# A weight column turned before the first block of x, and the mixer's first casts moved one unit later

## The chip, the cores and the metric

The kernel runs on one core of one Trainium2 chip. The metric is the device time of one execution in microseconds (us), as a median of runs. Every time in this document comes from such runs or from the profile of one execution.

Five engines work at the same time, each through its own list of instructions in order: PE (TensorE: matrix products and transposes), DVE (VectorE), ACT (ScalarE), POOL (GpSimd) and SP (SyncE, which only issues loads here). In the rows of the profile PEld is the loading of a stationary operand of PE, and SPq, ACTq and POOLq are DMA issues.

## The reference, cut to what matters

One layer of a residual block over 512 rows of 1024 features, all in float32:

```python
h = h + 0.5 * swiglu(rmsnorm(h, ffn1_norm), ffn1_w_in, ffn1_w_out)     # first layer, d_ff = 2816
z = rmsnorm(h, mix_norm) @ w_in                                        # the mixer's projection
h = h + concat([conv_module(z...), gated_linear_attention(z...)]) @ w_out
h = h + 0.5 * swiglu(rmsnorm(h, ffn2_norm), ffn2_w_in, ffn2_w_out)
h = h + sigmoid(rmsnorm(h, ple_norm) @ w_g) * (p @ w_p)
out = rmsnorm(h, final_norm)
```

The change touches the first rows (the norm's weight `ffn1_norm`) and the passage from the first layer to the mixer's projection.

## The kernel before, in words

Activations are kept transposed: eight tiles `hT` of 128 features by 512 rows. Each product is made of three: both operands are split into a high part in a rounded format (`wh`, `hg` high, `wa` high) and the rest (`wl`, `hg` low), and high by high, high by low and low by high are summed in PSUM. So each block of weights costs a cast on ACT (the high part) and a subtraction on DVE (the low part). For some blocks the low part is made in another way, by the helper `added`: ACT writes the negated high part, and a DMA issued by POOL adds the raw weights to it in place ("the add" below, `wa<-wr` with POOLq in the rows). That takes work from DVE and gives it to POOL and the DMA engines.

**The opening.** `warm_up` (line 196) gives PE idle products, then `turn_x(0, turn_vec)` transposes the first block of x in four pieces, with the norm's weight row turned into a column (`turn`, line 183) between the second piece and the third. `split_x` then scales block 0 by that column into `hg` (ACT high, DVE low), and `take` begins the products with the first weights.

**The first layer.** `ffn` lists units of PE work, two accumulator halves at a time. For the last pair of columns (number 10) the units m5, m4 and m3 finish its accumulators. After m3, ACT copies half of the last accumulator out (`g<-pd`), DVE adds and scales it, ACT applies the silu (`s<-g`), DVE multiplies (`m<-u,s`), and ACT and DVE split it (`act`). The pieces of the second matrix follow: four column pairs n = 0, 2, 4, 6, each in two groups of rows. The second group of n = 0 is the first that needs the `act` of pair 10. After each column pair is done, DVE adds it to `hT`, ACT and DVE make the mixer's `hg` of these two blocks, and ACT squares them.

**What sets the order.** PE, DVE and ACT keep the order in which the code emits them (class `Ordered`, line 36); `drive` (line 667 on) emits each unit's casts some units ahead of its products. `hooks` (line 1033 on) hang extra work on units: `ahead` (line 271) loads two blocks of mixer weights, casts them (`high4`, line 276) and starts their adds. It hangs on m4 of pair 10 (two blocks, called W0 and W1 here) and on the piece called ("last", 4) (two more, W2 and W3). Behind the layer `in_order(True)` (line 1053) starts a new chain, and the casts of four more mixer blocks, B0, B1 (`raw_b`) and A0, A1 (`raw_a`, from line 1105 on), are scheduled among the layer's last instructions by a scheduler of the framework; they may come before an earlier written instruction on ACT.

**Slots.** All raw weights share six slots `wr`. SP issues the loads in written order, and each waits until the last reader of a freed slot is done. For a block with `added` the last reader is the add itself; for others it is DVE's subtraction.

Of the kernel before, what the change touches and what calls it, by code (L numbers as in the profile page):

```python
# [15 lines left out]
P = 128  # L16
SEQ = 512
D = 1024
DC = D // P
DFF = 2816  # L20
D_CONV = 512
# [41 lines left out]
def block_kernel(ctx: ExitStack, tc: tile.TileContext, a: dict, out: bass.AP):  # L63
    nc = tc.nc
# [25 lines left out]
    def bt2(dt=F32R, s="a"):  # L90
        t = big.tile([P, 2, SEQ], dt, tag="A", bufs=NA, name=nm(s))
        hi, lo = t[:, 0], t[:, 1]
        whole_of[id(hi)] = hi, t
        return hi, lo
# [32 lines left out]
    def bank():  # L127
        if mode[0] == 0:
            turn_no[0] += 1
            at = turn_no[0] % 7  # L130
            if at in (3, 4):
                return fixed()
            if at in (5, 6):
                return spare()
        return psum(singles(), 3, [P, SEQ])
# [16 lines left out]
    def aux():  # L152
        if mode[0] == 2:
            return fixed()
        return psum(singles(), 1, [P, SEQ], "aux")
# [11 lines left out]
    vecs = [("ffn1_norm", 8), ("mix_norm", 8), ("ffn2_norm", 8), ("ple_norm", 8),  # L167
            ("conv_b", 4), ("conv_ln_g", 4), ("conv_ln_b", 4), ("gate_b", 2), ("gla_norm", 4)]
# [3 lines left out]
    def columns(names, n, tile_name, queue):  # L172

        row = cp.tile([n, P], F32, name=tile_name + "r")
        col = cp.tile([P, n], F32, name=tile_name)
        r0 = 0
        for name, m in names:
            queue.dma_start(out=row[r0:r0 + m, :], in_=a[name][0].rearrange("(r p) -> r p", p=P))
            for c in range(m):
                vcols[name, c] = col[:, r0 + c:r0 + c + 1]  # L180
            r0 += m

        def turn():
            ps = aux()
            pe.transpose(ps[:, 0:n], row, ident[:n, :n])
            dve.tensor_copy(col, ps[:, 0:n])

        return turn
# [7 lines left out]
    def warm_up(n, zeroed=0):  # L196
        idle = bank()
        for _ in range(zeroed):
            pe.matmul(idle[:, 0:P], zeros, zeros, start=True, stop=True)
        for _ in range(n):  # L200
            pe.transpose(idle[:, 0:P], ident, ident)

    warm_up(7, 2)
    turn_vec = columns(vecs[:1], 8, "vcol1", nc.scalar)

    def split(src, s, alloc=bt):
        hi, lo = bt2(s=s) if alloc is bt else (alloc(F32R, s + "H"), alloc(F32R, s + "L"))
# [20 lines left out]
    def raw(nk, ncol):  # L228
        return wp.tile([P, 1024], F32, tag="raw", bufs=6, name=nm("wr"))[:, :nk * ncol].rearrange(
            "p (k c) -> p k c", k=nk)  # L230

    def fetch(r3, src, k0, nk, c0, ncol):
        nc.sync.dma_start(out=r3, in_=src[k0 * P:(k0 + nk) * P, c0:c0 + ncol].rearrange("(k p) c -> p k c", p=P))

    def load(src, k0, nk, c0, ncol):
        r3 = raw(nk, ncol)
        fetch(r3, src, k0, nk, c0, ncol)
        return r3
# [16 lines left out]
    def added(w):  # L255

        h3, l3, r3 = w
        act.mul(l3, r3, -1.0)
        pool.dma_start(out=l3.bitcast(F32), in_=r3, accum_op=ALU.add)
        return w  # L260
# [10 lines left out]
    def ahead(src, c0, ncol):  # L271


        return [[added(w) for w in high4(load(src, 0, DC, c, P))] for c in range(c0, c0 + ncol, P)]

    def high4(r3):

        w = []
        for k in range(0, DC, 4):
            hi, lo = (t.rearrange("p (k c) -> p k c", k=4) for t in bt2(s="wa"))  # L280
            act.copy(hi, r3[:, k:k + 4])
            w.append((hi, lo, r3[:, k:k + 4]))
        return w
# [247 lines left out]
    def turn_x(c, between=None):  # L531
        ps = bank()
        for t in range(TB):
            if between and t == 2:
                between()
            pe.transpose(ps[:, t * P:(t + 1) * P], xt[c][t], ident)
        xps.append(ps)
# [64 lines left out]
    nc.sync.dma_start(out=made[1], in_=a["conv_w"][0])  # L602
    for i in range(P // RANK):
        nc.sync.dma_start(out=made[2][i * RANK:(i + 1) * RANK, :], in_=a["gate_w_up"][0])
    turn_x(0, turn_vec)
    warm_up(4)
    ps0 = [fixed(), fixed()] + parted(double())
    split_w(0, 1, dve.tensor_copy, 2)
# [30 lines left out]
    def constants():  # L639
        _, cwrow, gwurow = made  # L640
        gwu = cp.tile([P, 2 * P], F32, name="gwu")
        act.copy(gwu, gwurow)
        cw = cp.tile([P, 4 * WIDTH], F32, name="cw")
        ps = aux()
        for c in range(4):
            pe.transpose(ps[:, c * WIDTH:(c + 1) * WIDTH], cwrow[:, c * P:(c + 1) * P], ident[:WIDTH, :WIDTH])
        dve.tensor_copy(cw, ps[:, 0:4 * WIDTH])
        mean = cp.tile([P, P], F32, name="mean")
        pool.memset(mean, 1.0 / D_CONV)
        m1, m2 = (bt(s="m1")[:, 0:4 * CH].rearrange("p (c t) -> p c t", t=CH) for _ in range(2))  # L650
        mask = cp.tile([P, 4, CH], I32, name="mask")
        pool.memset(m1, 1.0)
        pool.memset(m2, 1.0)
        pool.affine_select(out=m1, in_=m1, compare_op=ALU.is_gt, fill=0.0, base=0,
                           pattern=[[0, 4], [-1, CH]], channel_multiplier=1)
        pool.affine_select(out=m2, in_=m2, compare_op=ALU.is_gt, fill=0.0, base=-CH,
                           pattern=[[0, 4], [-1, CH]], channel_multiplier=1)
        pool.tensor_copy(mask[0:CH], m1[0:CH])
        pool.tensor_copy(mask[CH:P], m2[CH:P])
        nbias = cp.tile([P, 2], F32, name="nbias")  # L660
        for j in range(2):
            dve.tensor_scalar(nbias[:, j:j + 1], vec("gate_b", j), -1.0, None, ALU.mult)
        made[:] = cw, gwu, mean, mask, nbias
# [359 lines left out]
    w_in = a["w_in"][0]  # L1023
    w_ahead = []

    def sums_hooks(x, names, at):

        h = {}
        for name, key in zip(names, at):
# [6 lines left out]
                  ("h4", 1): lambda *_: [steps[4](), xb.split("t2")],  # L1036
                  ("h5", 1): lambda *_: [xb.split("t3"), w2.s12()]})
    hooks.update({("m5", 3): lambda *_: made[0](), ("m3", 3): lambda *_: constants(),
                  ("m4", 10): lambda *_: w_ahead.append(ahead(w_in, D_CONV, 2 * P)),
                  ("last", 4): lambda *_: w_ahead.append(ahead(w_in, 0, 2 * P))})  # L1040
    FAR = {("h5", 1): 3, ("m1", 2): 3}
    CASTS = {("h5", 1): 4, ("m1", 2): 4}
# [78 lines left out]
    rs, rsb = mid  # L1121
# [427 lines left out]
    for k in range(4):  # L1549
        for n in range(3):  # L1550
            w, ps = half[n]
# [329 lines left out]
    rs = norm.rows()  # L1881
# [98 lines left out]
```

## Time and profile before

| what | value |
|---|---|
| median of 3 runs | 934.87 us (934.66 to 935.77) |
| the profiled execution's own time | 934.95 us |
| its span in the profile | 933.1 us |
| granted clock of PE | 0.997 |
| DMA queues | q1: loads issued by SP; q0: DMAs issued by POOL |

A row of the timeline has the start in us, the time from the start of the first to the end of the last of the instructions merged in it, the engine, the line, the operation, `out<-in` by the program's names, the shape, the count, and in brackets the idle time of the engine before it with what ended it. Nearly all compute rows have line 46, since the class `Ordered` records them; the tile names tell them apart. A row of DMA issues has the time that the issuing engine took, not the transfer.

### The profile page before, as it was taken

What the parts mean: (1) busy time and instruction counts of PE and PEld (TensorE: products, weight loads), DVE (VectorE), ACT (ScalarE), POOL (GpSimd) and SP (SyncE); (2) the same over time, 40 slices, a digit from 0 to 9 for tenths busy, and PEclk for the clock granted to TensorE, in tenths of its full rate; (3) what the DMA queues carried; (4) which work ended last, traced back from release to release, by engine and by line L of the source; (5) the groups of instructions that cost most, each with busy time, mean ns of one, the idle gap of its engine ahead of it and who ended that gap; (6) DMA issues with size and microseconds to landing.
All of it is one profiled execution on the core that took longest, in us unless ns stands there. A gap on an engine that the chain in (4) does not pass through costs nothing.

```text
span 933.1 us, 12990 instructions
## 1 busy us (share of the span) xinstructions
PE 923.0 (99%) x5011; PEld 785.3 (84%) x5011; DVE 826.6 (89%) x1107; ACT 509.7 (55%) x745; POOL 56.9 (6%) x74
## 2 busy tenths in 40 slices
PE   9999999999999999999999999999999999999996
PEld 7898888888888878788877889888888888888885
DVE  6799989999999776999987789999999999997896
ACT  5874445445544574463564875355445444456883
POOL 0100100000000021001030020000000000000131
PEclk9999999999999999999999999999999999999998
DMA  7643333233432594346552654333223422348463
GB/s 231 186 112 113 116 113 113 74 108 113 124 87 66 153 237 116 77 111 161 137 124 79 158 115 134 113 113 116 89 90 122 126 89 79 110 132 245 92 111 115
DMA packets 108129, 114.37 MB, mean 123 GB/s; under 512 B 5203, under 2 KB 96517, under 8 KB 108068
## 3 DMA queue, kind: packets, MB, share of 16 engines
q1 hardware_dynamic: 101748, 94.67, 33.0%
q0 software_dynamic: 6304, 18.88, 11.2%
q8 instruction: 39, 0.64, 0.3%
q14 instruction: 22, 0.18, 0.1%
q10 hardware_dynamic: 16, 0.00, 0.0%
HBM read 93.61 MB, written 2.10 MB: 103 GB/s over the span
## 4 chain that ended last, share of the span: by engine, by line
PE 96%; DVE 2%; ACT 1%; DMA 1%; issue 0%; POOLq 0%; DVEq 0%; ACTq 0%
PE ps L46 58%; PE pd L46 38%; DMA wr<-in_w_in 1%; DVE wl L46 1%; DVE sq L46 0%; DVE g L46 0%; ACT act L46 0%; ACT wa L46 0%; ACT wh L46 0%; DVE u L46 0%; DVE rs L46 0%; ACT yc L46 0%; DVE y L46 0%; DVE s L46 0%; DVE act L46 0%
## 5 line engine op out<-in xcount | busy, mean ns | idle before, releaser
L46 DVE TENSOR_TENSOR wl<-wr,wh 128x1024 fp32r<-128x1024 f32 (+2 forms) x161 | 188.6, 1182 | 18.6 <-ACT wh L46 18.5
L46 ACT CAST wh<-wr 128x1024 fp32r<-128x1024 f32 (+2 forms) x178 | 176.4, 1022 | 21.6 <-PE ps L46 6.4
L46 PE MATMUL pd<-hg,wh 128*128 128x512 f32 x576 | 150.0, 391 | 0.0
L46 PE MATMUL ps<-act,wh 128*128 128x512 f32 x448 | 138.8, 391 | 0.5 <-ACT act L46 0.3
L46 PEld LDWEIGHTS pd<-hg,wh 128*128 128x128 f32 x576 | 106.1, 188 | 20.7 <-DVE u L46 0.3
L46 PE MATMUL ps<-hg,wh 128*128 128x512 f32 (+1 forms) x448 | 117.7, 347 | 0.1
L46 PE MATMUL pd<-t,wh 128*128 128x512 f32 x392 | 98.3, 393 | 0.0
L46 PEld LDWEIGHTS ps<-act,wh 128*128 128x128 f32 x448 | 83.1, 188 | 17.7 <-ACT act L46 0.7
L46 ACT ACTIVATE s<-g 128x512 f32<-128x512 f32 x48 | 30.3, 632 | 117.7 <-DVE g L46 117.7
L46 ACT COPY sq<-pd 128x1024 f32<-128x1024 f32 x45 | 45.8, 1017 | 86.7 <-PE pd L46 52.4
L46 PEld LDWEIGHTS ps<-hg,wh 128*128 128x128 f32 x448 | 78.0, 190 | 11.7 <-issue 1.3
L46 PE MATMUL ps<-act,wl 128*128 128x512 f32 x224 | 87.2, 389 | 0.0
L46 PE MATMUL pd<-hg,wl 128*128 128x256 f32 (+1 forms) x544 | 83.9, 289 | 0.0
L46 PEld LDWEIGHTS pd<-hg,wl 128*128 128x128 f32 x544 | 75.9, 190 | 6.3
L46 PEld LDWEIGHTS pd<-t,wh 128*128 128x128 f32 x392 | 70.6, 189 | 12.5
L46 PE MATMUL ps<-hg,wl 128*128 128x512 f32 (+1 forms) x224 | 77.1, 344 | 0.0
L46 ACT CAST wh<-sm 128x1024 fp32r<-128x1024 f32 x42 | 44.1, 1051 | 57.1 <-DVE sm L46 50.9
L46 DVE SCALAR_TENSOR_TENSOR cv<-glu,cw,cv 128x502 f32<-128x502 f32 (+24 forms) x90 | 61.9, 734 | 0.3
L46 PEld LDWEIGHTS pd<-t,wl 128*128 128x128 f32 x392 | 53.5, 191 | 3.8
L46 DVE TENSOR_TENSOR sq<-pd,sq 128x1024 f32<-128x1024 f32 x45 | 54.8, 1219 | 0.8 <-PE pd L46 0.8
L46 DVE TENSOR_TENSOR wl<-sm,wh 128x1024 fp32r<-128x1024 f32 x42 | 51.1, 1220 | 5.0 <-ACT wh L46 5.0
L46 PE MATMUL ps<-wh,hg 128*128 128x512 f32 x176 | 54.8, 393 | 0.0
(322 smaller groups left out, 1638.5 us busy)
## 6 DMA issues: line engine op xcount, KB each, us to landing
wr<-in_ffn_w_in SPq DMA_DIRECT2D x84, 512.0 KB
wr<-in_ffn_w_out SPq DMA_DIRECT2D x32, 512.0 KB
wr<-in_w_in SPq DMA_DIRECT2D x20, 512.0 KB
wl<-wr POOLq DMA_DIRECT2D x18, 512.0 KB, 5.2
wr<-in_ffn_w_out SPq DMA_DIRECT2D x16, 384.0 KB
wr<-in_w_out SPq DMA_DIRECT2D x8, 512.0 KB
wq<-in_ple_w_gate SPq DMA_DIRECT2D x8, 512.0 KB
wl<-wq POOLq DMA_DIRECT2D x8, 512.0 KB, 4.6
```

Source lines behind the costliest of these rows:

```text
L46: inst = call(*args, **kwargs)
```

## The change

Three edits:

1. The column of the first norm's weight is turned right after the idle products, ahead of all four pieces of x, and the identity turns of `warm_up` ahead of it go from seven to five.
2. The hook on m4 of pair 10 now only loads W0 and W1. Casting them and starting their adds is moved to the hook on m3 of pair 10, one unit later.
3. `ahead` is cut into loading and `prepared`, which casts; for W2 and W3 it does the same work as before.

```diff
-    warm_up(7, 2)
-    turn_vec = columns(vecs[:1], 8, "vcol1", nc.scalar)
+    warm_up(5, 2)
+    columns(vecs[:1], 8, "vcol1", nc.scalar)()
...
-        return [[added(w) for w in high4(load(src, 0, DC, c, P))] for c in range(c0, c0 + ncol, P)]
+        return prepared([load(src, 0, DC, c, P) for c in range(c0, c0 + ncol, P)])
+
+    def prepared(rs):
+
+        return [[added(w) for w in high4(r3)] for r3 in rs]
...
-    turn_x(0, turn_vec)
+    turn_x(0)
...
-                  ("m4", 10): lambda *_: w_ahead.append(ahead(w_in, D_CONV, 2 * P)),
+                  ("m4", 10): lambda *_: w_ahead.append([load(w_in, 0, DC, D_CONV + i * P, P) for i in range(2)]),
+                  ("m3", 10): lambda *_: w_ahead.append(prepared(w_ahead.pop())),
```

The order of PE differs only in the opening, and those of DVE and POOL do not differ. ACT differs in two places. The first is the end of the first layer. Of the names, `wa_3028` and `wa_3030` belong to W0 and `wa_3038` and `wa_3040` to W1, `g_537` is the copy out of the last accumulator, and the `wh` of 768 are blocks of the second matrix. ACT before:

```order
L46 CAST wa_3028<-wr_3026 128x512
L46 CAST wa_3030<-wr_3026 128x512
L46 ACTIVATE wa_3028<-wr_3026 128x512
L46 ACTIVATE wa_3030<-wr_3026 128x512
L46 CAST wa_3038<-wr_3036 128x512
L46 CAST wa_3040<-wr_3036 128x512
L46 ACTIVATE wa_3038<-wr_3036 128x512
L46 ACTIVATE wa_3040<-wr_3036 128x512
L46 CAST wh_3048<-wr_2942 128x768
L46 COPY g_537_3068<-pd_2842 128x512
```

ACT at the same place after the change:

```order
L46 CAST wh_3030<-wr_2940 128x768
L46 COPY g_533_3050<-pd_2840 128x512
L46 CAST wa_3054<-wr_3024 128x512
L46 CAST wa_3056<-wr_3024 128x512
L46 ACTIVATE wa_3054<-wr_3024 128x512
L46 ACTIVATE wa_3056<-wr_3024 128x512
L46 CAST wa_3062<-wr_3026 128x512
L46 CAST wa_3064<-wr_3026 128x512
L46 ACTIVATE wa_3062<-wr_3026 128x512
L46 ACTIVATE wa_3064<-wr_3026 128x512
```

The eight instructions of W0 and W1 moved behind a weight cast and behind the copy out of the last accumulator.

The second place on ACT is in the making of the mixer's `hg`, just before the mixer begins. Here `wh_3317` is the cast of A0, `wh_3355` (after the change `wh_3353`) that of A1, and the `hg` are the high parts of blocks 2 and 3 and then 4. ACT before:

```order
L46 CAST wh_3317<-wr_3305 128x1024
L46 ACTIVATE hg_3200<-h_104,vcol 128x512
L46 ACTIVATE hg_3203<-h_105,vcol 128x512
L46 ACTIVATE sq_3207<-h_104 128x512
L46 ACTIVATE sq_3210<-h_105 128x512
L46 CAST wh_3355<-wr_3307 128x1024
L46 ACTIVATE hg_3232<-h_106,vcol 128x512
```

ACT at the same place after the change:

```order
L46 CAST wh_3315<-wr_3303 128x1024
L46 ACTIVATE hg_3198<-h_105,vcol 128x512
L46 CAST wh_3353<-wr_3305 128x1024
L46 ACTIVATE hg_3201<-h_106,vcol 128x512
L46 ACTIVATE sq_3205<-h_105 128x512
L46 ACTIVATE sq_3208<-h_106 128x512
L46 ACTIVATE hg_3230<-h_107,vcol 128x512
```

The cast of A1 moved ahead of the `hg` of block 3 and of two squares; the diff names none of these.

The third place is SP. Its loads stand in the same order, but slots come free in another order, so the waits of the loads differ. The rows are, in order, W2, W3, B0, B1, A0 and A1; DVE is a subtraction that reads the old block in the slot, DMASW with a number is an add (two for each block: 2 and 3 of W0, 4 and 5 of W1, 6 and 7 of W2), and DMAHW is the slot's earlier load. SP before:

```order
L233 DMA wr_3127<-in_w_in 128x8x128 [waits DMASW3_49,DMAHW7_49,DMASW2_49,Activation_49]
L233 DMA wr_3137<-in_w_in 128x8x128 [waits DMAHW4_49,DVE_49]
L233 DMA wr_3301<-in_w_in 128x8x128 [waits DMAHW0_49,DMASW5_49,DMASW4_49]
L233 DMA wr_3303<-in_w_in 128x8x128 [waits DMAHW5_49,DVE_49]
L233 DMA wr_3305<-in_w_in 128x8x128 [waits DMAHW6_49,DVE_49]
L233 DMA wr_3307<-in_w_in 128x8x128 [waits DMASW7_49,DMAHW2_49,DMASW6_49,Activation_49]
```

SP after the change:

```order
L233 DMA wr_3125<-in_w_in 128x8x128 [waits DMAHW4_49,DVE_49]
L233 DMA wr_3127<-in_w_in 128x8x128 [waits DMASW3_49,DMAHW7_49,DMASW2_49,Activation_49]
L233 DMA wr_3299<-in_w_in 128x8x128 [waits DMAHW5_49,DVE_49]
L233 DMA wr_3301<-in_w_in 128x8x128 [waits DMAHW0_49,DMASW5_49,DMASW4_49]
L233 DMA wr_3303<-in_w_in 128x8x128 [waits DMAHW6_49,DVE_49]
L233 DMA wr_3305<-in_w_in 128x8x128 [waits DMASW7_49,DMAHW2_49,DMASW6_49,Activation_49]
```

W2 no longer waits for the adds of W0, W3 does; B0 no longer waits for the adds of W1, B1 does. A1 waits for the adds of W2 in both.

## The prediction

> **What bounds the kernel now.** I read first the page's chain of work that ended last, then the waits of PE's weight loads over the whole span.
>
> ```profile
> PE 96%; DVE 2%; ACT 1%; DMA 1%; issue 0%; POOLq 0%; DVEq 0%; ACTq 0%
> ...
> PEld ps L46 <- ACT act L46: 0.7, 1, 0.7
> PEld ps L46 <- DVE act L46: 0.5, 1, 0.5
> PEld ps L46 <- DVE hg L46: 0.4, 1, 0.4
> ```
>
> PE carries 96% of the chain, so only what starts PE earlier or lets it wait moves the end. Three waits bear on the change. Two are on `act`, the split output of pair 10, at the end of the first layer. The third is on `hg`, the mixer's input, some 25 us later: small now, but it says that DVE delivers `hg` just when PE asks for it. PE's timeline at the first place, the end of m3 and then the second group of the piece n = 0:
>
> ```profile
> 321.31 1.12 PE L46 MATMUL pd<-hg,wl 128*128 128x256 f32 x8
> ...
> 330.46 0.62 PE L46 MATMUL ps<-act,wh 128*128 128x512 f32 x2
> ...
> 332.86 0.63 PE L46 MATMUL ps<-act,wh 128*128 128x512 f32 x2
> ```
>
> Six products start between 330.46 and 332.86. The 27 products of PE's row further below take 6.52 with their small waits, under 0.24 each, so six need at most 1.4 and took 2.40: **1.0 us lost**. The reason stands in ACT's timeline:
>
> ```profile
> 318.84 1.14 ACT L46 CAST wa<-wr 128x512 fp32r<-128x512 f32 x2 [2.42 <-DMA wr<-in_w_in]
> 319.89 1.15 ACT L46 ACTIVATE wa<-wr 128x512 fp32r<-128x512 f32 x2
> 324.15 1.14 ACT L46 CAST wa<-wr 128x512 fp32r<-128x512 f32 x2 [3.11 <-DMA wr<-in_w_in]
> 325.19 1.15 ACT L46 ACTIVATE wa<-wr 128x512 fp32r<-128x512 f32 x2
> 326.25 0.82 ACT L46 CAST wh<-wr 128x768 fp32r<-128x768 f32 x1
> 326.97 0.57 ACT L46 COPY g<-pd 128x512 f32<-128x512 f32 x1
> ...
> 330.89 1.14 ACT L46 CAST act<-m 128x512 fp32r<-128x512 f32 x2 [0.84 <-DVE m L46]
> 331.94 0.83 ACT L46 CAST wh<-wr 128x768 fp32r<-128x768 f32 x1
> 333.46 1.14 ACT L46 CAST wa<-wr 128x512 fp32r<-128x512 f32 x2 [0.69 <-DMA wr<-in_w_in]
> ```
>
> m3 ended at 322.43, but ACT stood at the cast of W1 until its load landed at 324.15, and copied the accumulator only at 326.97. `act` came at 330.89.
>
> **The change, part 1: the opening.**
>
> ```profile
> 2.14 1.70 PE L46 MATMUL ps<-ident 128*128 128x128 f32 x7
> 5.12 0.69 ACT L46 ACTIVATE hg<-ps,vcol 128x512 fp32r<-128x512 f32 x1 [2.19 <-PE ps L46]
> 8.46 0.69 ACT L46 ACTIVATE hg<-ps,vcol 128x512 fp32r<-128x512 f32 x1 [0.22 <-PE ps L46]
> ```
>
> Seven identity turns take 1.70, so about 0.21 each; two fewer give 0.43. The small turn of the column costs the same wherever it stands. So x's turns end 0.43 earlier and the first `hg` starts at 4.69. The second `hg` waits 0.22 behind a weight cast that itself waits for a load, so only about 0.3 gets through: I take **-0.3**. The ends are -0.43 and, if the column's row lands as late as PE now reads it (the turn stands behind two pieces of x), +0.4.
>
> **Part 2: the copy ahead of W0 and W1.** In ACT's new order the copy starts as m3 ends, 322.45. Eight `wa` instructions follow at 0.525 each (two rows, 318.84 and 319.89, hold four and are 1.05 apart): W0 from 322.93, W1 from 325.03, done at 327.13. Then a weight cast (0.82), DVE's subtraction and product (0.9 and 0.7), and `act` at 329.5 instead of 330.89. PE asks for it at 331.14, so the stall goes: **-1.0**, between 0 and -1.0. Alone, parts 1 and 2 give 933.6. What is late next is `hg`.
>
> **Part 3: the DMAs that move with the casts.** The adds of W0 and W1 move later, and the waits of SP's loads change (the order of SP). Issues of POOL and SP before:
>
> ```profile
> 320.81 1.78 POOL L46 DMA_DIRECT2D wa<-wr  x2 [204.20 <-ACT wa L46]
> 335.43 1.75 POOL L46 DMA_DIRECT2D wa<-wr  x2 [7.57 <-ACT wa L46]
> 327.59 0.37 SPq L233 DMA_DIRECT2D wr<-in_w_in  x1
> 333.79 1.30 SPq L233 DMA_DIRECT2D wr<-in_w_in  x1
> 344.05 0.37 SPq L233 DMA_DIRECT2D wr<-in_w_in  x1
> ```
>
> The three SP rows are the loads of W2, A0 and A1 (W3, B0 and B1 go out between the first two). An add follows the first cast of its block by 1.97 (318.84 to 320.81, and 333.46 to 335.43). The share of the two queues in three stretches tells how loads (q1) and adds (q0) meet. The first two rows are 329.4 to 331.2 (1.8 us), the third is 335.0 to 339.4, the last two 339.6 to 345.0 (5.4 us):
>
> ```profile
> q0 software_dynamic: 109, 0.22, 94.0%
> q1 hardware_dynamic: 89, 0.05, 13.0%
> q1 hardware_dynamic: 2527, 1.28, 116.0%
> q0 software_dynamic: 566, 1.03, 105.5%
> q1 hardware_dynamic: 162, 0.07, 6.0%
> ```
>
> In the first stretch W1's adds (issued before) ran, and loads issued after them got 0.05 MB. In the second, W2's adds, issued at 335.43, got nothing until the loads issued before them were through. So in this trace what is issued first goes first, and a load behind an add crawls at 0.03 MB/us. An add alone moves 0.19 MB/us, that is 2.75 us for a block of 0.52 MB; beside a crawling load 0.12, that is 4.3. A load runs at 0.29 to 0.31, 1.75 us a block, and lands some 0.5 later.
>
> Now the new order. W2's load waits only for a DVE subtraction whose cast now stands ahead of m3's copy; I put the load near 324.0, some 1.5 us behind the end of m3, through by 327. W0's adds (issued 324.9) run 327.0 to 329.8, W1's (327.0) to 332.8. W3 and B0 go out near 330.3, B1 at 333.2 when W1's adds have landed, A0 behind it near 333.8. ACT casts W2 from 331.3 (its load landed long ago), so its adds are issued at 333.3, 2.1 earlier than before: together with B1, and ahead of A0. That is the turn: before, A0 was issued 1.6 ahead of W2's adds. W3 and B0 end near 336.1, B1 near 337.9; then W2's and W3's adds (W3's issued at 337.3, since W3 lands near 335 and its casts start then) run for two times 4.3, to 346.5, with A0 crawling beside them: 0.24 MB. The rest takes 0.9; A0 lands near 348.0. A1, released by W2's adds near 342.7, follows A0 and lands near **349.6**. If these adds run alone first, A1 lands near 347.0.
>
> **Part 4: the cast of A1 ahead of block 3's `hg`.** The rows of before are three of ACT, two of DVE and one of PE, at the mixer's start:
>
> ```profile
> 344.62 1.33 ACT L46 ACTIVATE hg<-h,vcol 128x512 fp32r<-128x512 f32 x2
> 345.86 1.14 ACT L46 ACTIVATE sq<-h 128x512 f32<-128x512 f32 x2
> 348.36 1.05 ACT L46 CAST wh<-wr 128x1024 fp32r<-128x1024 f32 x1 [1.36 <-DMA wr<-in_w_in]
> 346.18 1.41 DVE L46 SCALAR_TENSOR_TENSOR hg<-h,vcol,hg 128x512 fp32r<-128x512 f32 x2
> ...
> 355.53 1.42 DVE L46 SCALAR_TENSOR_TENSOR hg<-h,vcol,hg 128x512 fp32r<-128x512 f32 x2 [0.20 <-ACT hg L46]
> 351.93 6.52 PE L46 MATMUL ps<-hg,wa 128*128 128x512 f32 x27
> ```
>
> A1's cast waited 1.36 for its load at 348.36, behind the `hg` of blocks 2 and 3, and cost nothing. Now block 3's `hg` and two squares stand behind it, and DVE, which takes them in order, behind those. DVE finished block 3 at 347.59 and block 6 at 356.28 (355.53 and half a pair), 8.7 us of nearly unbroken work, and PE used block 6 at once. If A1's cast starts at L, block 3's `hg` starts on ACT at L + 0.95, is done on DVE at L + 2.45, and block 6 at L + 11.15. So PE is late by **L - 345.1** against now, and the 1.0 of part 2 is spent in that wait. With L = 349.6 that is +4.5. The ends: L cannot lie under about 346.4, since from 332.8 on the DMA engines owe W3, B0, B1, A0 and A1 (five times 1.75) and at least W2's adds (2.75) plus part of W3's: +1.3. Over 350 B1 must be late too (second rival).
>
> Everything behind the mixer's first products, DVE's chain included, waits for these `hg`, and PE has no load to wait for later that would take the delay in.
>
> **Sum** against the profiled execution (span 933.1, its time 934.95, the median 0.08 below): -0.3 + 4.5 with the stall's 1.0 inside the wait, so +4.2: 934.87 + 4.2 = **939.1 us**.
>
> **Rivals.**
> - *W2's adds still queue behind B1 and A0*, as they did in the stretch to 339.4. Then adds run 339.7 to 342.4, A1 goes out at 342.8 behind W3's adds, and lands near 347.0: 347.0 - 345.1 - 0.3 = +1.6, **936.5**. For it: SP's B1 is so close; against it: A0's issue itself took 1.30 when the queue was full.
> - *B1 falls behind the adds as well.* Then it crawls until 345 and lands near 346.2; ACT casts B1 ahead of block 0's `hg`, which then starts at 347.2. Going on in the same way (block 2 at 350.9, the cast of A1 at 351.5) gives L = 351.5 and +6.1: **941.0**. It decides if W2's adds go out 0.3 earlier or W1's land 0.3 later than worked out. [...]
> - *Not slower.* If the loads run ahead of all adds and A1 lands by 344, its cast hides behind block 2's `hg`, and parts 1 and 2 remain: -1.3, **933.6**. Above 345.1 it turns into a loss. Against it: the sum of transfers above.
>
> **How the numbers follow.** The forecast has 0.41, W2's adds behind B1 and A0 0.22, B1 late too 0.20, not slower 0.15, anything else 0.02. The bound of what a measurement tells is 0.2%, 1.87 us: 936.74 and 933.0. Slower takes the forecast, the late B1 and a third of the second rival (L over 347.3): 0.69. Faster by over 0.2% would need more than both gains together (1.0 + 0.43), so 0.02; the rest is 0.29. The range leaves out the upper end of the late B1 and most of not slower: 935.4 to 941.4.
>
> **What would show it.** Right: no `act` wait of PE near 331; W2's adds at about 333 in POOL's row; a cast of 128x1024 with a long wait for `wr<-in_w_in` between two single `hg` of ACT near 349; PE waiting several us for `hg` at the mixer's start. Wrong: that cast starting before 346, or PE going through the mixer's first 27 products without a wait.

## The result, and the profile after the change

The changed kernel takes **939.84 us** (median of 6 runs, 939.08 to 940.86), the kernel before 934.61 in the runs beside it (934.23 to 935.77). The ratio is 1.0055, with a 95% interval from 1.0042 to 1.0068: slower by 5.2 us. The profiled execution of the changed kernel took 940.86 us, with a span of 939.1; it is the longest of the six, and that matters below.

First the chain of work that ended last, from the page of the changed kernel:

```profile
PE 98%; DVE 1%; ACT 0%; issue 0%; POOLq 0%; DVEq 0%
```

Then the waits of PE's weight loads from 300 to 400 us, where the kernel before had the three waits on `act` and `hg`:

```profile
PEld ps L46 <- issue: 8.4, 13, 4.5
```

And the waits of PE's products from 320 to 370 us:

```profile
PE ps L46 <- DVE h L46: 4.1, 1, 4.1
```

The waits on `act` are gone, and one wait of about 4 us is there instead. PE's timeline shows where: between the last product of the first layer and the first of the mixer.

```profile
350.69 0.39 PE L46 MATMUL ps<-act,wl 128*128 128x512 f32 x1
355.19 9.28 PE L46 MATMUL ps<-hg,wa 128*128 128x512 f32 x27 [4.10 <-DVE h L46]
```

The mixer starts at 355.19 instead of 351.93. That is 3.3 us later, but it is not all: its first 27 products take 9.28 us instead of 6.52. They end 6.0 us later than before, and the span is 6.0 longer. The second loss stands in the table of stretches. Its columns are the stretch, its length, the busy time and in brackets the instructions of PE, PEld, DVE, ACT and POOL, then PE's granted clock, the share of the DMA engines and GB/s:

```profile
351.00:354.40 3.40, 0.08 (x1) 0.00 (x0) 3.40 (x6) 0.76 (x2) 0.00 (x0) 1.00 0.90 247
354.50:357.90 3.40, 2.71 (x7) 2.16 (x8) 3.10 (x5) 2.35 (x4) 0.00 (x0) 0.50 0.50 156
357.90:361.30 3.40, 3.40 (x10) 2.63 (x8) 3.21 (x6) 2.38 (x4) 0.00 (x0) 0.50 0.00 0
361.40:364.50 3.10, 3.10 (x17) 2.56 (x15) 0.75 (x2) 0.00 (x0) 0.00 (x0) 1.00 0.00 0
```

PE stood still for 4.1 us, and its clock was at half for 6.8 us: 10 products in the 3.4 us of the third row, against 14 of the same kind (and three short ones) in the 3.1 us of the fourth.

The reason for the wait is again in ACT's timeline:

```profile
322.53 0.59 ACT L46 COPY g<-pd 128x512 f32<-128x512 f32 x1 [4.90 <-PE pd L46]
...
329.64 1.14 ACT L46 CAST act<-m 128x512 fp32r<-128x512 f32 x2 [1.09 <-DVE m L46]
...
337.30 1.14 ACT L46 CAST wa<-wr 128x512 fp32r<-128x512 f32 x2 [3.69 <-DMA wr<-in_w_in]
...
343.16 1.05 ACT L46 CAST wh<-wr 128x1024 fp32r<-128x1024 f32 x1 [1.99 <-DMA wr<-in_w_in]
344.11 1.33 ACT L46 ACTIVATE hg<-h,vcol 128x512 fp32r<-128x512 f32 x2
...
347.32 1.05 ACT L46 CAST wh<-wr 128x1024 fp32r<-128x1024 f32 x1 [0.84 <-DMA wr<-in_w_in]
348.28 0.72 ACT L46 ACTIVATE hg<-h,vcol 128x512 fp32r<-128x512 f32 x1
349.04 1.05 ACT L46 CAST wh<-wr 128x1024 fp32r<-128x1024 f32 x1
349.99 0.72 ACT L46 ACTIVATE hg<-h,vcol 128x512 fp32r<-128x512 f32 x1
```

The copy out of the last accumulator starts as m3 ends, and `act` comes at 329.64, as forecast (329.5). Then ACT stands three times at a cast whose load has not landed: W3 (337.30), B1 (343.16) and A0 (347.32). B1's cast stands ahead of block 0's `hg`, which comes at 344.11 instead of 340.83. ACT before:

```profile
340.83 1.33 ACT L46 ACTIVATE hg<-h,vcol 128x512 fp32r<-128x512 f32 x2
```

A0's cast stands ahead of block 2's, at 348.28 instead of 344.62. A1's cast, at 349.04, has no wait of its own and only adds to that: block 3's `hg` comes at 349.99. DVE follows:

```profile
344.86 1.42 DVE L46 SCALAR_TENSOR_TENSOR hg<-h,vcol,hg 128x512 fp32r<-128x512 f32 x2 [1.32 <-ACT hg L46]
...
350.75 0.75 DVE L46 SCALAR_TENSOR_TENSOR hg<-h,vcol,hg 128x512 fp32r<-128x512 f32 x1 [0.54 <-ACT hg L46]
...
353.76 1.28 DVE L46 SCALAR_TENSOR_TENSOR h<-pd,h 128x512 f32<-128x512 f32 x2
...
359.44 1.42 DVE L46 SCALAR_TENSOR_TENSOR hg<-h,vcol,hg 128x512 fp32r<-128x512 f32 x2 [0.20 <-ACT hg L46]
```

Block 6's `hg` stands at 359.44 instead of 355.53, 3.91 later. By the profile PE's first wait ends with the row at 353.76, in which DVE empties the accumulators of blocks 4 and 5; this fits if the mixer's accumulators take these places in PSUM, which no run here shows. In other traces below the profile names ACT's `hg` at the same place; both stand in the same late chain.

Why the loads are late stands in the issues of POOL (the adds of W2 and of W3) and of SP (the loads of W2, W3 with B0 behind it, B1 with A0 behind it, and A1). After the change:

```profile
333.39 1.75 POOL L46 DMA_DIRECT2D wa<-wr  x2 [4.58 <-ACT wa L46]
339.27 1.75 POOL L46 DMA_DIRECT2D wa<-wr  x2 [4.13 <-ACT wa L46]
```

```profile
324.05 0.37 SPq L233 DMA_DIRECT2D wr<-in_w_in  x1
330.42 1.89 SPq L233 DMA_DIRECT2D wr<-in_w_in  x2
334.05 3.08 SPq L233 DMA_DIRECT2D wr<-in_w_in  x2
341.79 0.37 SPq L233 DMA_DIRECT2D wr<-in_w_in  x1
```

The share of the two queues in three stretches, 334 to 335.8, 337.4 to 339.3 and 341.8 to 345 (packets, MB, busy share):

```profile
q1 hardware_dynamic: 1077, 0.54, 105.7%
...
q1 hardware_dynamic: 899, 0.46, 82.2%
q0 software_dynamic: 68, 0.11, 31.2%
...
q0 software_dynamic: 271, 0.50, 86.4%
q1 hardware_dynamic: 488, 0.24, 26.0%
```

Loads (q1) run alone for one block of 0.5 MB, then both queues move with the loads ahead, then the adds (q0) have most of it and a load crawls. So W2's adds, issued at 333.39, are served among the loads, not behind all of them and not ahead of them.

### The profile page after: what moved, and what is told of

The parts are those of the page before. It is cut to its first block, busy times and chain, and to the rows that moved or that the text cites. A ratio compares the mean times of both kernels' runs of the same rounds, so it can differ in the third digit from the quotient of the medians.

```text
span 939.1 us, 12986 instructions
## 1 busy us (share of the span) xinstructions
PE 925.4 (99%) x5009; PEld 787.1 (84%) x5009; DVE 826.9 (88%) x1107; ACT 509.8 (54%) x745; POOL 56.8 (6%) x74
## 4 chain that ended last, share of the span: by engine, by line
PE 98%; DVE 1%; ACT 0%; issue 0%; POOLq 0%; DVEq 0%
PE ps L46 59%; PE pd L46 39%; DVE sqacc L46 0%; DVE h L46 0%; ACT wh L46 0%; DVE u L46 0%; DVE rs L46 0%; ACT yc L46 0%; DVE y L46 0%; DVE g L46 0%; DVE s L46 0%; DVE hg L46 0%; DVE lnsq L46 0%; ACT hg L46 0%; POOLq L1981 0%
```

## The experiments

A short diff stands with each; where nothing else is said it is against the changed kernel. Ratios are against the kernel before on the same chip.

**Which edit carries the loss.** The second edit alone, with the opening of the kernel before:

```diff
-    warm_up(5, 2)
-    columns(vecs[:1], 8, "vcol1", nc.scalar)()
+    warm_up(7, 2)
+    turn_vec = columns(vecs[:1], 8, "vcol1", nc.scalar)
...
-    turn_x(0)
+    turn_x(0, turn_vec)
```

> Only the second edit of the change (W0 and W1 cast and their adds started one unit later); the opening is as before. Theory A, read from the changed kernel's trace: the whole loss comes from this edit, and the opening gives nothing (its work stands 0.07 us later at 99 us). Then the time is that of the changed kernel within 0.5 us, 939.3 to 940.3. The prediction's opening term of -0.3 would put it 0.3 above the changed kernel, at 940.1. Rival: the opening takes part in the loss; then it is clearly below, near 935.

Measured: 939.21 us (938.15 to 940.71), ratio 1.0049 [1.0037, 1.0062]. The loss is there without the new opening. PE's row in its trace:

```profile
354.34 4.76 PE L46 MATMUL ps<-hg,wa 128*128 128x512 f32 x19 [3.01 <-DVE h L46]
```

The wait is there, a little shorter, and the 19 products behind it take 0.24 each: in this execution the clock did not fall.

The first edit alone, against the kernel before:

```diff
-    warm_up(7, 2)
-    turn_vec = columns(vecs[:1], 8, "vcol1", nc.scalar)
+    warm_up(5, 2)
+    columns(vecs[:1], 8, "vcol1", nc.scalar)()
...
-    turn_x(0, turn_vec)
+    turn_x(0)
```

> The kernel before with the first edit alone (five identity turns instead of seven, the column turned ahead of x). The prediction's term is -0.3: 0.3 below the kernel before. Reading of the changed kernel's trace: x's turns end 0.4 earlier, but the products behind them lose 0.53 at two places and stand 0.02 ahead at 6.4 us, so within 0.1 of no change, 934.4 to 934.6. A rival from five traces so far: at 99 us the work of the kernels with the new opening stands at -0.03 to +0.54 of the kernel before, 0.26 in the mean; then it is 0.3 above.

Measured: 934.04 us (933.30 to 935.95), ratio 0.9995 [0.9986, 1.0003]: no difference that can be told, and below the 934.4 to 934.6 that was expected. What the new opening does to the first products is seen in DVE's and PE's timelines of the changed kernel, the high part of the first weights and the first real products:

```profile
4.29 0.29 DVE L46 CAST wh<-wr 128x256 fp32r<-128x256 f32 x1 [0.48 <-DMA wr<-in_ffn_w_in]
5.39 0.29 DVE L46 CAST wh<-wr 128x256 fp32r<-128x256 f32 x1 [0.81 <-DMA wr<-in_ffn_w_in]
```

```profile
5.43 0.80 PE L46 MATMUL ps<-hg,wh 128*128 128x512 f32 x1
6.03 0.54 PE L46 MATMUL pd<-hg,wh 128*128 128x512 f32 x1
6.41 0.40 PE L46 MATMUL ps<-hg,wh 128*128 128x512 f32 x1
...
99.19 0.40 PE L46 MATMUL ps<-actL,wh 128*128 128x512 f32 x1
```

The first product starts at 5.43, but the next two wait, since the second half of the first weights lands only at 5.39. The third stood at 6.43 before and stands at 6.41 now. The row at 99.19 is a landmark: it lies between 98.96 and 99.54 in five traces with the old opening (99.24 in the mean) and between 98.75 and 99.67 in nine with the new one (99.34). So the traces show no gain from the opening: x is ready earlier, but the first weights' load ends last. The times leave room for the predicted 0.3, since the interval reaches from -1.3 to +0.3 us.

**Is it the place of A1's cast?** One order on ACT is added:

```diff
+    block3 = act.log[-9]
...
     w2a.append(high(raw_a[1]))
+    act.behind(act.latest, block3)
```

> The changed kernel, with one order added on ACT: the cast of A1 stands behind block 3's hg and its squares, as before the change. The prediction's part 4 put the wait of PE down to that place of the cast. If that holds, the wait of 4.3 us at the mixer's start goes and with it the slow products behind it: 933.9. Rival, read from the changed kernel's trace: B1 and A0 land late themselves, so that DVE's hg of block 0 is 3.16 late (344.86 against 341.70) and that of block 2 is 3.28 late (349.46 against 346.18) ahead of A1's cast, and only 0.6 of block 3's 3.86 is A1's place: 939.3 at most 0.7 below the changed kernel, or some 2 us lower where the shorter wait no longer slows the products behind it.

Measured: 938.06 us (937.71 to 938.36), ratio 1.0037 [1.0024, 1.0049]. Two thirds of the loss stay, so the place of A1's cast is not the cause by itself. The time lies between the two cases of the rival. PE in its trace, and then the stretch behind its wait:

```profile
353.23 8.02 PE L46 MATMUL ps<-hg,wa 128*128 128x512 f32 x27 [2.24 <-ACT hg L46]
```

```profile
354.60:357.90 3.30, 3.30 (x10) 2.52 (x9) 3.00 (x6) 1.48 (x3) 0.00 (x0) 0.50 0.10 37
```

PE still waits for `hg`, because B1's and A0's casts stand ahead of blocks 0 and 2. The clock fell although PE had stood for only 2.24 us, but for 3.4 us and not for 6.8: from 358 on it is at 1.00.

**Is it ACT standing at late casts, or the late transfers themselves?** All four casts of B0 to A1 go behind the last square of block 7 on ACT:

```diff
+    block7 = act.last
...
     in_order(True)
+    act.last = block7
```

> The changed kernel, with the casts of all four blocks B0, B1, A0 and A1 behind the last square of block 7 on ACT; DVE's subtractions for B0, B1 and A0 then move behind its hg too. Theory: the wait of PE is made by ACT, which stands at casts of weights that land late ahead of hg that need none of them. Then PE neither waits near 331 nor at the mixer's start, and the 1.0 of the stall is gained: 933.9, or 933.4 with the small hg wait of 0.4 gone as well. Rival: the late transfers themselves or the mixer's later weights cost the time (the four casts and three subtractions now stand ahead of the norm's last steps on DVE): 936 or more.

Measured: 933.96 us (933.42 to 934.65), ratio 0.9993 [0.9984, 1.0003]. The whole loss is gone. PE and ACT in its trace:

```profile
351.34 6.28 PE L46 MATMUL ps<-hg,wa 128*128 128x512 f32 x27
```

```profile
336.81 1.14 ACT L46 CAST wa<-wr 128x512 fp32r<-128x512 f32 x2 [2.78 <-DMA wr<-in_w_in]
...
341.36 1.34 ACT L46 ACTIVATE hg<-h,vcol 128x512 fp32r<-128x512 f32 x2 [1.63 <-DVE h L46]
```

W3 still lands late (its casts start at 336.81), but block 0's `hg` waits only for its own input, and PE has no wait. So late weights cost nothing here; what costs is an `hg` queued behind their casts.

**What makes the loads late?** W2's and W3's adds are replaced by subtractions on DVE, with ACT's order unchanged:

```diff
-                  ("last", 4): lambda *_: w_ahead.append(ahead(w_in, 0, 2 * P))})
+                  ("last", 4): lambda *_: w_ahead.append([[by_dve(w) for w in high4(load(w_in, 0, DC, i * P, P))] for i in range(2)])})
...
+    def by_dve(w):
+
+        act.mul(w[1], w[2], -1.0)
+        low(w)
+        return w
```

> The changed kernel, with the low parts of W2 and W3 made by four subtractions on DVE instead of the four adds by DMA; ACT keeps all its instructions in their order (the negated copies of W2 and W3 are still written and then overwritten, a waste on purpose). Theory: B1, A0 and A1 are late because W2's and W3's adds go out among them and because A1's load waits for W2's adds. Without these adds W3, B0, B1, A0 and A1 need five times 1.75 us behind 333: B1 lands near 339, A0 near 340.5, A1 near 342.5, block 0's hg stands at 341 on ACT, and PE does not wait at the mixer's start: 933.9 to 934.5. Rival: the later adds of W0 and W1 alone make the loads late; then W3 still lands at 337.3, B1 past 340, and the time is 937 or more.

Measured: 935.65 us (935.27 to 936.29), ratio 1.0013 [1.0005, 1.0022]. Four of the five us go with these adds. ACT in its trace:

```profile
336.29 1.14 ACT L46 CAST wa<-wr 128x512 fp32r<-128x512 f32 x2 [2.23 <-DMA wr<-in_w_in]
...
341.02 1.33 ACT L46 ACTIVATE hg<-h,vcol 128x512 fp32r<-128x512 f32 x2
...
345.73 1.04 ACT L46 CAST wh<-wr 128x1024 fp32r<-128x1024 f32 x1
```

Block 0's `hg` is back at 341.02, and B1 and A0 make no wait. W3's casts still wait, to 336.29 (337.30 in the changed kernel): its load waits for W0's adds (the order of SP) and in the changed kernel it goes out at 330.42, instead of 328.09 in the kernel before. The edit takes away the traffic of these adds and A1's wait for W2's at once; that B1 and A0, which wait for no add of W2 or W3, are in time again points to the traffic. A1's cast still stands ahead of block 3's `hg`, at 345.73, which by the prediction's rule (start minus 345.1) costs 0.6.

Only W1 is moved behind m3's copy; W0 is cast in the hook on m4, as before the change:

```diff
-                  ("m4", 10): lambda *_: w_ahead.append([load(w_in, 0, DC, D_CONV + i * P, P) for i in range(2)]),
-                  ("m3", 10): lambda *_: w_ahead.append(prepared(w_ahead.pop())),
+                  ("m4", 10): lambda *_: w_ahead.append([load(w_in, 0, DC, D_CONV + i * P, P) for i in range(2)]) or w_ahead.append(prepared(w_ahead[0][:1])),
+                  ("m3", 10): lambda *_: w_ahead.append(w_ahead.pop() + prepared(w_ahead.pop()[1:])),
```

> The changed kernel, but only W1's casts and adds are moved behind m3's copy; W0 is cast in the hook on m4, as before the change. The loads then wait for the same things as before, and A1's cast stands behind block 3's squares. Theory: the loads are late because the adds of W0 (and those of W2 that follow) were pushed 4 us into them; with W0's adds back at 321, W3 lands before 333, the copy still starts at 322.5, PE has no stall near 331, and none at the mixer's start: 933.4 to 934.0. Rival: W2's casts come 2 us earlier than in the kernel before, since act does, and their adds go out ahead of A0's load; A0 is late, block 2's hg with it, and PE waits 1 to 3 us at the mixer's start: 935 to 937.

Measured: 935.06 us (934.23 to 937.24), ratio 1.0009 [1.0000, 1.0018]. Nearly all of the loss is gone with W0's adds back at 320.94, but the gain does not come. The median lies at the lower end of the rival's range, but the trace does not show the rival: W2's casts start at 333.12 and not 2 us earlier than the 333.46 of the kernel before. In the trace PE begins the mixer at 351.02, 0.9 earlier than before, and its second group there waits for `hg`, so part of the gain is given back:

```profile
356.02 2.12 PE L46 MATMUL ps<-hg,wa 128*128 128x512 f32 x8 [0.28 <-DVE hg L46]
```

**The slow products.** In the changed kernel PE gets 16 identity turns to do while it waits:

```diff
+    idle_bank = double()
...
+    idle = idle_bank[:, 0]
+    for _ in range(16):
+        pe.transpose(idle[:, 0:P], ident, ident)
     pb0 = zblock(wb[0], hg)
```

> The changed kernel with 16 identity turns (about 0.21 each, 3.4 us) on PE between the last product of the first layer and the mixer's first product, where PE waits 4.3 us; their result is not used. Theory: the 13 products at 0.427 instead of 0.227 behind that wait come from the granted clock, which the trace of the changed kernel shows at 0.50 from 354.5 to 361.3 because PE stood still before. With the turns it stays at 1.00, the products take 0.227, and PE is held back only by block 6's hg, some 3.9 late: about 938.2, 1.6 below the changed kernel, with less spread between the runs. Rival: the slow products come from something else (the late weights, the transfers), then they stay: 939.8.

Measured: 938.63 us (937.96 to 938.72), ratio 1.0041 [1.0029, 1.0054]. The stretch behind the wait, and PE:

```profile
354.90:358.00 3.10, 3.10 (x14) 2.58 (x15) 2.95 (x5) 1.67 (x4) 0.00 (x0) 1.00 0.36 136
```

```profile
354.90 4.77 PE L46 MATMUL ps<-hg,wa 128*128 128x512 f32 x19 [1.76 <-ACT hg L46]
```

The turns ran in 1.9 us instead of 3.4, which leaves a wait of 1.76; the clock stayed at 1.00, and the products take 0.24. So the slow products come from PE's standing still, and not from the late weights or the transfers. The rest, 3.9 us, is the late `hg`. The intervals of this run and of the changed kernel overlap, so the gain in time is not told from nothing.

The changed kernel once more, for a second trace (no diff):

> The changed kernel once more, for a second trace of it. If the slow products depend on where PE's wait falls in a fixed window of the granted clock, as 6.83 us at half clock in one trace, 3.41 in the trace with A1's cast moved back and none in the trace of the casts alone suggest, then this trace has 0, 3.4 or 6.8 us at half clock and no other length. If they belonged to the wait alone, it is 6.8 again.

Measured: one run of 938.02 us. PE, and the stretches:

```profile
353.69 7.86 PE L46 MATMUL ps<-hg,wa 128*128 128x512 f32 x27 [3.04 <-DVE h L46]
```

```profile
353.40:356.80 3.40, 3.11 (x7) 2.51 (x8) 3.10 (x6) 1.96 (x4) 0.00 (x0) 0.50 0.42 150
356.90:360.00 3.10, 3.10 (x15) 2.55 (x14) 2.87 (x5) 2.38 (x4) 0.00 (x0) 1.00 0.00 0
```

The clock is at half for one stretch of 3.4 us. So the same program pays 3.4 or 6.8 us at half clock, and its time moves with that: 940.86 with two such stretches, 938.02 with one (a wait 1.1 shorter and an opening 0.4 shorter are in that difference too). Since this run of the changed kernel is as low as the runs with the turns, the times alone do not settle what the slow clock costs in the median. The products lose 1.4 (7 of them, 0.2 each) to 2.8, but part of that PE would have waited for block 6's `hg` anyway. In this trace that `hg` is 2.4 later than in the kernel before:

```profile
357.95 1.42 DVE L46 SCALAR_TENSOR_TENSOR hg<-h,vcol,hg 128x512 fp32r<-128x512 f32 x2 [0.19 <-ACT hg L46]
```

The 27 products end 3.1 later, so the clock adds 0.7 here, and 2.1 in the first trace (6.0 less 3.9).

**The stall that was to be gained.** The kernel before once more, for a second trace (no diff):

> The kernel before once more, for a second trace of it. If the stall of 1.0 near 331 belongs to every execution, W1's cast starts near 324.15 (1.6 to 1.7 behind m3's last product) and PE loses about 1.0 at act again. If it comes and goes with the landing of W1's load, the cast starts 0.5 to 1.3 earlier against m3's end, and the stall is smaller or gone.

Measured: one run of 934.23 us. ACT and the waits of PE's weight loads from 300 to 400 us:

```profile
323.40 1.14 ACT L46 CAST wa<-wr 128x512 fp32r<-128x512 f32 x2 [2.49 <-DMA wr<-in_w_in]
...
330.14 1.14 ACT L46 CAST act<-m 128x512 fp32r<-128x512 f32 x2 [0.83 <-DVE m L46]
```

```profile
PEld ps L46 <- DVE act L46: 0.5, 1, 0.5
```

W1's cast, which waits for its load, started 0.75 earlier than in the first trace (m3 ended at the same time, 322.40), `act` came at 330.14 instead of 330.89, and one small wait is left of the stall: the six products from 330.42 on take 1.69 instead of 2.40, where 1.4 would do. In the trace of the opening alone, with ACT's order as before, W1's cast started at 322.85 and `act` at 329.59, and PE had no `act` wait. So the stall of 1.0 belongs to some executions only.

The casts of B0 to A1 behind block 7 in the kernel before, without both edits of the change:

```diff
+    block7 = act.last
...
     in_order(True)
+    act.last = block7
```

> The kernel before (both edits undone), with the casts of B0, B1, A0 and A1 behind the last square of block 7 on ACT. Against the two runs that have these casts there together with the moved W0 and W1 (933.96 and 933.86) it tells what the second edit itself is worth once its harm is taken away. The prediction's part 2 says 1.0: then this is 934.9, no better than the kernel before or 0.4 below it for the hg wait that goes. Rival: the stall near 331 is there in some executions only (it is missing in the trace of the opening alone, where W1's cast starts at 322.85 instead of 324.15 with ACT's order unchanged); then the second edit is worth less than 0.5, and this is 933.9 to 934.3.

Measured: 934.46 us (933.78 to 934.94), ratio 0.9999 [0.9990, 1.0008]. This is 0.5 above the same repair with W0 and W1 moved, half of what part 2 of the prediction says; the intervals overlap, so the 0.5 is not shown to differ from nothing. The time is that of the first expectation's lower case and above the rival's range, but the trace is the rival's: W1's cast starts at 322.38, 0.1 behind m3, and PE has no `act` wait. So of four traces with the casts of W0 and W1 in their old place one has the stall of 1.0, one has 0.3 of it and two have none.

**Versions that might beat both.** The casts behind block 7, with the opening of the kernel before:

```diff
-    warm_up(5, 2)
-    columns(vecs[:1], 8, "vcol1", nc.scalar)()
+    warm_up(7, 2)
+    turn_vec = columns(vecs[:1], 8, "vcol1", nc.scalar)
...
+    block7 = act.last
...
     in_order(True)
+    act.last = block7
```

> The kernel of the earlier run with all four casts behind block 7, but with the opening of the kernel before. That run was 0.5 below the kernel before, though its trace gains 1.47 between 99 and 455 us. Theory: the new opening took part of it (+0.3 in the mean of the traces); then this is 933.4 to 933.7. Rival: the opening is worth the predicted -0.3, then 934.3.

Measured: 933.86 us (933.59 to 934.43), ratio 0.9994 [0.9985, 1.0003], against 0.9993 with the new opening: no difference between the openings can be told.

Only W1 moved, and the casts behind block 7:

> The two repairs together: only W1's casts and adds moved behind m3's copy (W0 in the hook on m4 as before the change), and the casts of B0, B1, A0 and A1 behind the last square of block 7. Theory: PE meets no stall near 331 in any execution, since m3's copy waits for no load, and no hg wait at the mixer's start, since no cast of a late block stands ahead of an hg. Then the time is 933.4 to 933.9, below both kernels, with less spread than the run with W1 alone (934.23 to 937.24). Rival: that run's upper values come from somewhere else, and this one reaches above 935 too.

Measured: 934.10 us (933.46 to 934.34), ratio 0.9994 [0.9984, 1.0003]. As expected it reaches no value above 935, where the run with W1 alone has six of eleven: the spread goes away with the casts that wait ahead of an `hg`. Its median is 0.2 above the range expected. PE's first 27 products of the mixer take 6.28 in its trace, without a wait.

All three kernels with the repair and a moved W1 lie 0.5 to 0.8 us below the kernel before, on the same side, but each interval takes in 1. They beat the changed kernel by 0.6%, and the kernel before by no more than can be told.

## Why the prediction was right, and where it was not

The forecast was 939.1, the measured median 939.84, with the sign and the place as said. But the sum came out right partly by luck: it left out the half clock, and what it put down to A1's cast alone is the work of three casts.

- **Part 1, the opening, -0.3:** mis-sized. It measured 0.1 the other way in the landmark at 99 us, and 934.04 against 934.69 in time, which is not told from nothing. The 0.43 of the two identity turns came (the first `hg` starts at 4.69, as worked out; 0.21 is the distance of two turns' starts, while 1.70 divided by 7 is 0.24). The step that failed is the one that let the earlier end of x's turns through to the products: the first weights' load ends last, a wait that the one trace of before did not show.
- **Part 2, the stall, -1.0:** the mechanism is right (copy at 322.53, `act` at 329.64, no `act` wait). The size was that of one execution: a second trace of before loses 0.3 there, and two more traces with that order nothing. With the harm taken away the edit measures 0.5, not told from nothing.
- **Part 3, the order of the DMAs:** the issues were close: W3's load 330.42 (330.3), W2's adds 333.39 (333.3), B1's load 334.05 (333.2), A1's 341.79 (342.7). The start of A1's cast, 349.04, is near the 349.6 too, and the run without W2's and W3's adds shows that these carry four of the five us. Wrong was that W3, B0 and B1 run ahead of these adds undisturbed: W3's casts started at 337.30 instead of 335.3, and B1's at 343.16, with block 0's `hg` at 344.11 instead of 340.83. This is what the second rival ("B1 falls behind the adds as well") describes, and its condition held: W1's adds, for which B1's load waits, were through 0.85 later than worked out. Its size did not: B1 landed 3 us before that rival had it, which fits queues that share rather than wait for each other. In the two stretches from 337.4 on both queues move, though in the one from 334 on loads run alone (0.54 MB) beside adds issued at 333.39. The share in MB is not an even one: q0 gets 0.11 MB beside 0.46 in one stretch and 0.50 beside 0.24 in another.
- **Part 4, A1's cast:** the rule "late by L - 345.1" gives 3.94 for L = 349.04, and block 6's `hg` is 3.91 late. As a cause it failed: with A1's cast put back, two thirds of the loss stay, and only with B1's and A0's casts out of the way too does it vanish. A1's place was the last of three in a row. One of the signs named for a right forecast failed with it: the cast near 349 has no long wait for its load, the long waits stand at W3's, B1's and A0's casts.
- **The wait of PE:** the forecast has it at block 6's `hg`; it came at the first product, which by the profile waits 4.10 for DVE's emptying of PSUM, in the same late chain.
- **What no term held:** the half clock behind the wait, 7 to 14 products at 0.43 instead of 0.23. In the profiled execution block 6's `hg` accounts for 3.9 and the end of the mixer's first products is 6.0 late, so the clock adds 2.1 there, and 0.7 in the second trace of the changed kernel. Without it the forecast, corrected for L = 349.04 and for an opening that gives nothing, would have been 3.9 above the kernel before, as is the run with the turns.
- "Not slower" needed the loads ahead of all adds; no trace of the changed kernel shows it. "W2's adds still queue behind B1 and A0" would have had B1 in time, and it was not; that the queue was full while A0's issue took 1.30 was the author's reading, the row shows the 1.30 alone. The chances for slower add up to 0.68 and not 0.69, which changes nothing.

## What to carry to other kernels

Moving work off one engine's critical place also moves the transfers that it starts, here into the loads that the next casts on the same in-order engine wait for (W2's adds at 333.39 instead of 335.43, B1's cast at 343.16). Casts that are needed late belong behind the urgent work and not between its steps; there the late loads cost nothing in this kernel (933.96 us, against 939.84 with the casts between). A stall that ends with one load's landing may be 1.0 in one execution and nothing in the next (1.0, 0.3 and twice nothing in the four traces here), so a second trace is worth having before it is counted as a gain.

## What was unexpected

**The granted clock falls for 3.4 or 6.8 us, behind waits of 2.2 to 4.1.** It was at 0.50 behind waits of 4.10 (for 6.8 us), 3.04 and 2.24 (for 3.4 us), and stayed at 1.00 behind one of 3.01 and with the turns in the wait. So the length of the wait alone doesn't decide. All these falls last once or twice 3.4 us, as the first case of the expectation for the second trace of the changed kernel had it. In the other trace with a wait of 3.0 the clock did not fall at all, and no run shows what decides that.

**The landing of one load differs by more than a us between executions.** W1's cast started at 324.15, 323.40 and 322.85 with the same order ahead of it, and the second half of the first weights landed in time in one trace of the old opening and made DVE wait 0.4 to 0.65 in the four others.
